# Row softmax: nine-row tiles in ten buffers, stores issued from ScalarE, rows scaled one by one

## The chip, the cores and the metric

The kernel runs on one core of a Trainium2 chip. The metric is device time in microseconds (us); one profiled execution of each kernel gives a span, which is about 1.9 us shorter than the time (164.57 us against 162.7 us for the kernel before). A core has five instruction streams: VectorE (DVE), ScalarE (ACT), GpSimd (POOL), SyncE (SP, which only issues loads here) and TensorE (not used here). Each works through its own list in order. The page of a profile counts 16 DMA engines on the core, which move the data.

## The reference

16,384 rows of 512 floats, softmax with temperature 0.5 over each row:

```
x_scaled = x / 0.5
x_max = np.max(x_scaled, axis=-1, keepdims=True)
exp_x = np.exp(x_scaled - x_max)
return (exp_x / np.sum(exp_x, axis=-1, keepdims=True)).astype(np.float32)
```

That is 33.55 MB in and 33.55 MB out, with little arithmetic.

## The kernel before

128 partitions take 8 rows each, so a tile has 1024 rows (2 MiB) and there are 16 tiles. The row maximum is found on VectorE, the exponential and the row sum on ScalarE; of the 8 rows, 6 are scaled on VectorE in one instruction and 2 on ScalarE. Loads are issued by SyncE, stores by GpSimd.

```python
    G = 8
    ...
    data = ctx.enter_context(tc.tile_pool(name="data", bufs=8))
    stats = ctx.enter_context(tc.tile_pool(name="stats", bufs=8))
    ...
    for c in range(C):
        xt = data.tile([P, G, D], fp32, name="xt")
        nc.sync.dma_start(out=xt, in_=xr[c])
        negmax = stats.tile([P, G], fp32, name="negmax")
        nc.vector.reduce_max(negmax, xt, axis=AX, negate=True)
        sums = stats.tile([P, G], fp32, name="sums")
        for g in range(G):
            nc.scalar.activation(out=xt[:, g, :], in_=xt[:, g, :], func=EXP,
                                 bias=negmax[:, g : g + 1], scale=2.0,
                                 accum_out=sums[:, g : g + 1])
        recip = stats.tile([P, G], fp32, name="recip")
        nc.vector.reciprocal(recip, sums)
        ...   # rows 2 to 7: one tensor_mul on VectorE; rows 0 and 1: COPY with scale on ScalarE
        nc.gpsimd.dma_start(out=outr[c], in_=xt)
```

The library's scheduler decides, when the program is built, in which order the instructions stand on each engine. It keeps the data dependences, not the order of the source.

The softmax here doesn't subtract the row's maximum and nothing guards it: scores larger than these inputs give would overflow.

## Time and profile before

| | before |
|---|---|
| time, median of runs | 164.57 us (164.56 to 164.75, 3 runs) |
| span of the profiled run | 162.7 us |
| DMA over the span | 67.13 MB, 413 GB/s |
| VectorE, ScalarE busy | 77%, 69% |

First the page of the kernel before: busy time of each engine, then 40 equal slices of the span (4.07 us each; a digit is the busy share in tenths, GB/s is what the DMA engines moved), then the chain of work that ended last.

```profile
DVE 124.6 (77%) x48; ACT 112.5 (69%) x289; POOL 8.8 (5%) x20
...
DMA  5999999999999999999999999999999999979994
GB/s 161 431 431 427 431 439 334 411 433 443 423 423 443 431 419 443 439 415 439 443 411 433 443 423 423 443 431 419 439 443 415 435 443 415 431 318 447 407 431 193
...
DMA 61%; DVE 18%; ACT 8%; issue 6%; POOLq 0%; SPq 0%
...
L51 ACT ACTIVATE xt<-xt,negmax 128x512 f32<-128x512 f32 x128 | 90.5, 708 | 28.3 <-DVE negmax L47 28.3
L47 DVE TENSOR_REDUCE negmax<-xt 128x8 f32<-128x4096 f32 x16 | 70.5, 4406 | 25.6 <-DMA xt<-in_x_dram 25.6
L65 DVE TENSOR_TENSOR xt<-xt,recip 128x3072 f32<-128x3072 f32 x16 | 53.6, 3349 | 0.1
```

No engine is near full, the DMA row is full nearly everywhere, and DMA is 61% of the chain. Data movement bounds this kernel. In the lines of groups the two numbers after the bar are total busy us and mean ns of one; after the second bar stands the idle time before them and what ended it: VectorE's reductions wait for loads, ScalarE for the reductions. Two slices fall short: 334 GB/s where the first store begins, 318 GB/s near 145 us.

Next the timeline of VectorE in the middle of the kernel before (start, duration, engine, line, operation):

```profile
97.64 4.42 DVE L47 TENSOR_REDUCE negmax<-xt 128x8 f32<-128x4096 f32 x1 [1.91 <-DMA xt<-in_x_dram]
101.98 3.35 DVE L65 TENSOR_TENSOR xt<-xt,recip 128x3072 f32<-128x3072 f32 x1
105.25 0.20 DVE L61 RECIPROCAL recip<-sums 128x8 f32<-128x8 f32 x1
107.34 4.42 DVE L47 TENSOR_REDUCE negmax<-xt 128x8 f32<-128x4096 f32 x1 [1.90 <-DMA xt<-in_x_dram]
```

One reduction, one scaling, in turn, 9.7 us a tile: for every tile that is loaded one is stored.

### The profile page before, as it was taken

How to read it: one execution, taken by the hardware profiler on the slowest of the kernel's cores; microseconds unless marked ns; L12 is line 12 of the kernel's file. 1: busy time of each engine (PE TensorE's matmuls, PEld its weight loads, DVE VectorE, ACT ScalarE, POOL GpSimd, SP SyncE). 2: the span in 40 equal slices, each digit the busy share in tenths (PEclk: the TensorE clock that was granted, in tenths of full speed). 3: DMA queues.
4: the chain of work that ended last, by engine and by line, in shares of the span. 5: the costliest groups of instructions: out<-in, count | busy, mean ns of one | idle time of the engine just before them, and what ended most of it. 6: DMA issues, size and time to landing. Idle time of an engine off the chain costs nothing.

```text
span 162.7 us, 483 instructions
## 1 busy us (share of the span) xinstructions
DVE 124.6 (77%) x48; ACT 112.5 (69%) x289; POOL 8.8 (5%) x20
## 2 busy tenths in 40 slices
DVE  0098799999999979596993959969596895999200
ACT  0038997999999995939589294885939579396000
POOL 0000010010101010101001010010101001011100
DMA  5999999999999999999999999999999999979994
GB/s 161 431 431 427 431 439 334 411 433 443 423 423 443 431 419 443 439 415 439 443 411 433 443 423 423 443 431 419 439 443 415 435 443 415 431 318 447 407 431 193
DMA packets 4610, 67.13 MB, mean 413 GB/s; under 512 B 512, under 2 KB 512, under 8 KB 512
## 3 DMA queue, kind: packets, MB, share of 16 engines
q1 hardware_dynamic: 2304, 33.56, 49.2%
q0 software_dynamic: 2304, 33.56, 48.3%
q14 instruction: 2, 0.02, 0.0%
HBM read 33.55 MB, written 33.55 MB: 413 GB/s over the span
## 4 chain that ended last, share of the span: by engine, by line
DMA 61%; DVE 18%; ACT 8%; issue 6%; POOLq 0%; SPq 0%
DMA xt<-in_x_dram 40%; DMA out_dram<-xt 22%; DVE negmax L47 11%; ACT xt L51 7%; DVE xt L65 6%; ACT xt L71 1%; DVE recip L61 0%; POOLq L104 0%; SPq L44 0%; POOLq L78 0%
## 5 line engine op out<-in xcount | busy, mean ns | idle before, releaser
L51 ACT ACTIVATE xt<-xt,negmax 128x512 f32<-128x512 f32 x128 | 90.5, 708 | 28.3 <-DVE negmax L47 28.3
L47 DVE TENSOR_REDUCE negmax<-xt 128x8 f32<-128x4096 f32 x16 | 70.5, 4406 | 25.6 <-DMA xt<-in_x_dram 25.6
L65 DVE TENSOR_TENSOR xt<-xt,recip 128x3072 f32<-128x3072 f32 x16 | 53.6, 3349 | 0.1
L51 ACT ACTIVATION_READ_ACCUMULATOR xt<-xt,negmax 128x1 f32 x128 | 24.0, 187 | 0.0
L71 ACT ACTIVATE xt<-xt,recip 128x512 f32<-128x512 f32 x32 | 21.1, 707 | 0.3 <-DVE recip L61 0.3
L78 POOL DMA_DIRECT2D out_dram<-xt x16 | 8.6, 540 | 143.5 <-ACT xt L51 89.3
L51 ACT ACT_TABLE_LOAD x1 | 1.3, 1283 | 8.4 <-DMA xt<-in_x_dram 8.4
L61 DVE RECIPROCAL recip<-sums 128x8 f32<-128x8 f32 x16 | 3.1, 195 | 1.2 <-ACT xt L51 1.2
L93 POOL MEMSET const-float32-0.0<- 128x1 f32 x1 | 0.1, 98 | 0.2 <-issue 0.2
L93 POOL MEMSET const-bfloat16-1.0<- 128x1 bf16 x1 | 0.1, 101 | 0.0
L93 POOL MEMSET const-float32-1.0<- 128x1 f32 x1 | 0.1, 98 | 0.0
L93 POOL MEMSET const-uint8-127<- 128x1 uint8 x1 | 0.1, 98 | 0.0
## 6 DMA issues: line engine op xcount, KB each, us to landing
xt<-in_x_dram SPq DMA_DIRECT2D x16, 2048.0 KB, 28.8
out_dram<-xt POOLq DMA_DIRECT2D x16, 2048.0 KB, 17.0
```

Source lines behind the costliest of these rows:

```text
L47: nc.vector.reduce_max(negmax, xt, axis=AX, negate=True)
L51: nc.scalar.activation(out=xt[:, g, :], in_=xt[:, g, :], func=EXP, bias=negmax[:, g : g + 1], scale=2.0, accum_out=sums[:, g : g + 1],)
L61: nc.vector.reciprocal(recip, sums)
L65: nc.vector.tensor_mul(xt[:, k:, :], xt[:, k:, :], recip[:, k:].unsqueeze(2).broadcast_to((P, G - k, D)),)
L71: nc.scalar.activation(out=xt[:, g, :], in_=xt[:, g, :], func=COPY, scale=recip[:, g : g + 1],)
L78: nc.gpsimd.dma_start(out=outr[c], in_=xt)
L93: nc = _bacc.Bacc("TRN2", target_bir_lowering=False, num_devices=1)
```

## The change

The intent: fewer and larger transfers (15 tiles; 9 rows are an 18 KiB piece of HBM for each partition), more of them in flight (ten buffers), a short last tile (2 rows) for a short end, a simpler split of work (ScalarE only exponentials, VectorE all scaling, row by row, in an instruction form that was expected to be faster), and stores from a hardware queue instead of GpSimd's software queue.

```diff
-    G = 8
-    C = N // (P * G)
+    GMAX = 9
+    R = N // P
+    sizes = [GMAX] * (R // GMAX)
+    if R % GMAX:
+        sizes.append(R % GMAX)
 ...
-    data = ctx.enter_context(tc.tile_pool(name="data", bufs=8))
-    stats = ctx.enter_context(tc.tile_pool(name="stats", bufs=8))
+    data = ctx.enter_context(tc.tile_pool(name="data", bufs=10))
+    stats = ctx.enter_context(tc.tile_pool(name="stats", bufs=4))
+    warm = stats.tile([P, 1], fp32, name="warm", bufs=1)
+    nc.vector.memset(warm, 0.0)
+    nc.scalar.activation(out=warm, in_=warm, func=EXP)   # loads the exponential's table early
 ...
-        nc.vector.reduce_max(negmax, xt, axis=AX, negate=True)
+        nc.vector.tensor_reduce(negmax, xt, axis=AX, op=mybir.AluOpType.max, negate=True)
+        bias = stats.tile([P, G], fp32, name=f"bias{G}")
+        nc.vector.tensor_scalar_mul(bias, negmax, 2.0)
 ...
-        if N_ACT_NORM < G: ... tensor_mul of rows 2 to 7 on VectorE
-        for g in range(N_ACT_NORM): ... COPY with scale of rows 0 and 1 on ScalarE
-        nc.gpsimd.dma_start(out=outr[c], in_=xt)
+        for g in range(G):
+            nc.vector.tensor_scalar_mul(xt[:, g, :], xt[:, g, :], recip[:, g : g + 1])
+        nc.scalar.dma_start(out=outr, in_=xt)
```

More of the change, by code (lines that the diff above doesn't have):

```diff
@@ L19 @@
     P = nc.NUM_PARTITIONS
+    AX = mybir.AxisListType.X
+    EXP = mybir.ActivationFunctionType.Exp
     D = x.shape[-1]
@@ L24 @@
     N = xf.shape[0]
-    G = 8
-    C = N // (P * G)
-    assert C * P * G == N
-    N_ACT_NORM = 2
-    xr = xf.rearrange("(c p g) d -> c p g d", p=P, g=G)
-    outr = of.rearrange("(c p g) d -> c p g d", p=P, g=G)
-    data = ctx.enter_context(tc.tile_pool(name="data", bufs=8))
-    stats = ctx.enter_context(tc.tile_pool(name="stats", bufs=8))
-    AX = mybir.AxisListType.X
-    EXP = mybir.ActivationFunctionType.Exp
-    COPY = mybir.ActivationFunctionType.Copy
-    for c in range(C):
-        xt = data.tile([P, G, D], fp32, name="xt")
-        nc.sync.dma_start(out=xt, in_=xr[c])
-        negmax = stats.tile([P, G], fp32, name="negmax")
-        nc.vector.reduce_max(negmax, xt, axis=AX, negate=True)
-        sums = stats.tile([P, G], fp32, name="sums")
+    GMAX = 9
[3 more added lines that the diff above has]
+        sizes.append(R % GMAX)
+    assert sum(sizes) * P == N
+    data = ctx.enter_context(tc.tile_pool(name="data", bufs=10))
[3 more added lines that the diff above has]
+    nc.scalar.activation(out=warm, in_=warm, func=EXP)
+    row = 0
+    for G in sizes:
+        xr = xf[row : row + P * G, :].rearrange("(p g) d -> p g d", g=G)
+        outr = of[row : row + P * G, :].rearrange("(p g) d -> p g d", g=G)
+        row += P * G
+        xt = data.tile([P, G, D], fp32, name=f"xt{G}", bufs=10 if G == GMAX else 1)
+        nc.sync.dma_start(out=xt, in_=xr)
+        negmax = stats.tile([P, G], fp32, name=f"negmax{G}")
+        nc.vector.tensor_reduce(negmax, xt, axis=AX, op=mybir.AluOpType.max, negate=True)
+        bias = stats.tile([P, G], fp32, name=f"bias{G}")
+        nc.vector.tensor_scalar_mul(bias, negmax, 2.0)
+        sums = stats.tile([P, G], fp32, name=f"sums{G}")
         for g in range(G):
@@ L54 @@
                 func=EXP,
-                bias=negmax[:, g : g + 1],
+                bias=bias[:, g : g + 1],
                 scale=2.0,
@@ L58 @@
             )
-        recip = stats.tile([P, G], fp32, name="recip")
+        recip = stats.tile([P, G], fp32, name=f"recip{G}")
         nc.vector.reciprocal(recip, sums)
-        if N_ACT_NORM < G:
-            k = N_ACT_NORM
-            nc.vector.tensor_mul(
-                xt[:, k:, :],
-                xt[:, k:, :],
-                recip[:, k:].unsqueeze(2).broadcast_to((P, G - k, D)),
-            )
-        for g in range(N_ACT_NORM):
-            nc.scalar.activation(
-                out=xt[:, g, :],
-                in_=xt[:, g, :],
-                func=COPY,
-                scale=recip[:, g : g + 1],
-            )
-        nc.gpsimd.dma_start(out=outr[c], in_=xt)
+        for g in range(G):
+            nc.vector.tensor_scalar_mul(xt[:, g, :], xt[:, g, :], recip[:, g : g + 1])
+        nc.scalar.dma_start(out=outr, in_=xt)
 _INS = ['x']
```

## The prediction

> **What bounds it now.** Data movement. The profile's slices show 411 to 447 GB/s from 4 us to 158 us, except two dips (334 and 318 GB/s); 67.1 MB over the 162.7 us span is 413 GB/s. One load plus one store takes 9.71 us (spacing of the VectorE reductions late in the timeline) = 432 GB/s. VectorE is busy 77%, ScalarE 69%; both wait for loads in mid-kernel. The chain of waits is 61% DMA. What isn't streaming: about 3 us of start, about 1 us lost at the first store, about 1.2 us near 145 us when stores come one by one, and about 2 us of end. So about 5 us at most can be won, by better feeding.
>
> **What the change does, costed.**
> - VectorE: the reduction grows from 4.42 us (8 rows) to about 4.95 (9). Scaling 6 rows in one 3.35 us tensor_tensor becomes 9 one-row tensor_scalar. The Trainium skill, "VectorE: DVE Perf Modes", section "The perf-mode tier table", gives fp32 tensor_scalar twice the rate of tensor_tensor (1227 ns for 2048 elements); my estimate from it for 512 is 0.42 us alone, 0.35 back to back, so 3.1 us for nine. Total VectorE work: about 120 us, little changed.
> - ScalarE loses 32 scaling passes (21.1 us) and gains 15 store issues, estimated at 0.1 to 0.5 us each (load issues take 0.35). The table load moves earlier; it was already hidden.
> - Stores leave the software queue. The Trainium skill, "DMA: Bandwidth & Descriptors", section "Issuing engines are not separate DMA queues", says all issuers share the same engines, so I expect no rate gain; loads and stores split the 432 GB/s evenly in this trace too. It should save the dip at the first store (about 1 us).
> - 18 KiB pieces instead of 16: no rate change expected.
>
> **The main effect: the instruction order.** The built order of the changed kernel is no longer one reduction, one scaling. VectorE reduces tiles 10, 11 and 12 before it scales tile 6, and 14 and 15 before it scales tile 8. Load 12 waits for store 2. ScalarE, which now issues the stores in order, stands still at store 6 until that scaling is done, and its exponentials stand still with it. Adding the trace's durations along this order (5.46 us per 2.25 MiB at 432 GB/s, halves when loads and stores overlap): load 12 lands near 96 us, store 6 is issued near 105, all loads have landed by about 110, store 8 is issued near 122. Eight tiles' stores remain, only seven of them full, with nothing to overlap: each needs nine exponentials (9 x 0.704 = 6.34 us) and an issue, 6.4 to 6.9 us on ScalarE, against 5.46 us of data movement. The queues run dry for about 4 us near 120 to 124 us and 1 to 1.4 us after each later store: about 12 us idle in all, against about 1 before.
>
> **Predicted:** 175 us, range 169 to 179. Faster by over 2%: 0.03; within 2%: 0.10; slower by over 2%: 0.87.
>
> **What would show it.** Slices full until about 110 us, then GB/s near 340 to 370 to the end; ScalarE waiting for VectorE's scaling before stores 3 to 8 (longest wait over 10 us, near store 6), then busy without gaps from about 122 us; ScalarE's last full tiles 6.4 to 6.9 us apart; tensor_scalar near 0.42 us each; row stores landing in the tail about 6.7 us apart.
>
> **What would make it wrong.** Loads taking more than half of the bandwidth beside hardware-queue stores (store 8 earlier: about 6 us less); scaling at single rate, 0.6 us a row (about 15 us more); a store issue on ScalarE hidden or much dearer than 0.4 us (2 us either way); a real gain in rate from 18 KiB pieces.

## The result, and the profile after

The changed kernel takes 176.1 us (176.04 to 176.17, 4 runs) against 164.56 us (164.41 to 164.75, 4 runs): a ratio of 1.0709, with a 95% interval of 1.0688 to 1.073. Ratios here are the mean time of one kernel's runs over that of the other's of the same rounds, so not quite the ratio of the quoted medians. It is slower by 7%.

The page of the changed kernel, the same parts as above (a slice is 4.35 us here):

```profile
DVE 125.3 (72%) x174; ACT 93.5 (54%) x258; POOL 0.2 (0%) x4
...
DMA  6999999999999999999999999959097798798796
GB/s 186 419 453 419 419 457 318 432 432 449 413 436 436 415 438 432 432 441 419 436 436 419 436 432 415 451 229 407 0 436 311 339 407 339 339 407 339 339 407 256
...
DMA 39%; DVE 31%; ACT 21%; issue 3%; ACTq 0%; DVEq 0%; SPq 0%
...
L60 ACT ACTIVATE xt<-xt,bias 128x512 f32<-128x512 f32 x128 | 90.5, 708 | 68.2 <-DVE xt L72 39.2
L54 DVE TENSOR_REDUCE negmax<-xt 128x9 f32<-128x4608 f32 (+1 forms) x15 | 70.4, 4700 | 22.1 <-DMA xt<-in_x_dram 22.1
L72 DVE TENSOR_SCALAR xt<-xt,recip 128x512 f32<-128x512 f32 x128 | 52.0, 480 | 0.2
```

VectorE's total is the same as before and ScalarE has 19 us less to do, yet the kernel is slower. Up to about 110 us the DMA rows of both kernels look alike. After that the changed kernel has a slice of 0 and then a pattern of 339, 339, 407. The chain has moved from DMA to VectorE and ScalarE. The next two windows of the trace say how much that is (length, busy time of VectorE, ScalarE and GpSimd, clock, DMA share, GB/s). First the kernel before:

```profile
4.00:110.00 106.00, 89.14 (x34) 83.24 (x215) 5.45 (x10) 1.00 1.01 427
110.00:161.00 51.00, 35.44 (x15) 29.24 (x74) 3.19 (x6) 1.00 0.98 416
```

And the changed kernel:

```profile
4.00:110.00 106.00, 85.61 (x85) 48.24 (x134) 0.00 (x0) 1.00 1.01 427
110.00:173.00 63.00, 39.64 (x89) 43.79 (x122) 0.00 (x0) 1.00 0.80 337
```

At 110 us both have moved the same bytes at 427 GB/s. Both then have 21.2 MB left (51 x 416 and 63 x 337). At the 432 GB/s of the steady state that takes 49.1 us: the kernel before loses 1.9 us on it, the changed one 13.9 us. The difference, 12.0 us, accounts for the loss of the change (the spans differ by 11.4 us).

What differs at 110 us is *which* bytes have moved. The queues up to that time (packets, MB, share), the kernel before, loads first, then stores:

```profile
q1 hardware_dynamic: 1937, 28.33, 61.7%
q0 software_dynamic: 1200, 17.56, 37.3%
```

The changed kernel, loads first, then stores:

```profile
q1 hardware_dynamic: 2160, 33.56, 72.8%
q10 hardware_dynamic: 749, 12.33, 26.1%
```

The changed kernel has loaded everything and stored little more than a third. From here it can only store, as fast as tiles become ready. Why the stores fell behind stands in VectorE's timeline of the changed kernel:

```profile
76.99 3.65 DVE L72 TENSOR_SCALAR xt<-xt,recip 128x512 f32<-128x512 f32 x9
80.56 4.95 DVE L54 TENSOR_REDUCE negmax<-xt 128x9 f32<-128x4608 f32 x1
87.94 4.95 DVE L54 TENSOR_REDUCE negmax<-xt 128x9 f32<-128x4608 f32 x1 [2.44 <-DMA xt<-in_x_dram]
98.14 4.95 DVE L54 TENSOR_REDUCE negmax<-xt 128x9 f32<-128x4608 f32 x1 [5.25 <-DMA xt<-in_x_dram]
...
103.25 3.65 DVE L72 TENSOR_SCALAR xt<-xt,recip 128x512 f32<-128x512 f32 x9
```

Between the scaling of tile 5 (76.99 us) and that of tile 6 (103.25 us) stand three reductions, of tiles 10, 11 and 12, and two of them wait for their loads. (Pairs of reductions stand ahead of the scalings of tiles 2, 3 and 4 too, and ScalarE has waited 6.57, 11.91 and 7.10 us at stores 3, 4 and 5 before that.) ScalarE has the store of tile 6 in its own list, ahead of the rest of tile 8's exponentials, and stands still with it (ACTq lines are ScalarE issuing a store):

```profile
80.67 0.34 ACTq L74 DMA_DIRECT2D out_dram<-xt  x1
...
106.94 0.34 ACTq L74 DMA_DIRECT2D out_dram<-xt  x1
107.32 0.72 ACT L60 ACTIVATE xt<-xt,bias 128x512 f32<-128x512 f32 x1 [13.46 <-DVE recip L70]
...
125.49 0.34 ACTq L74 DMA_DIRECT2D out_dram<-xt  x1
...
132.07 0.34 ACTq L74 DMA_DIRECT2D out_dram<-xt  x1
...
138.65 0.34 ACTq L74 DMA_DIRECT2D out_dram<-xt  x1
```

No store was issued for 26 us, and ScalarE idled 13.46 us of them in one piece. The label of that wait, a reciprocal on VectorE, names only the nearest event: the store was issued at 106.94 us, just as the scaling of tile 6 ended (103.25 + 3.65 = 106.90). From store 8 at 125.49 us on, stores come every 6.58 us. In that time ScalarE does nine exponentials (nine times 0.704 us, the spacing of their starts, is 6.34 us) and issues a store. A full tile's store needs 5.46 us of data movement at 432 GB/s. So the DMA engines idle between stores.

### The profile page after: what moved, and what is told of

The parts are those of the page before. It is cut to its first block, busy times and chain, and to the rows that moved or that the text cites. A ratio compares the mean times of both kernels' runs of the same rounds, so it can differ in the third digit from the quotient of the medians.

```text
span 174.1 us, 533 instructions
## 1 busy us (share of the span) xinstructions
DVE 125.3 (72%) x174; ACT 93.5 (54%) x258; POOL 0.2 (0%) x4
## 3 DMA queue, kind: packets, MB, share of 16 engines
q1 hardware_dynamic: 2160, 33.56, 46.0%
q10 hardware_dynamic: 2160, 33.56, 45.3%
## 4 chain that ended last, share of the span: by engine, by line
DMA 39%; DVE 31%; ACT 21%; issue 3%; ACTq 0%; DVEq 0%; SPq 0%
DMA xt<-in_x_dram 30%; ACT xt L60 21%; DVE negmax L54 18%; DVE xt L72 13%; DMA out_dram<-xt 9%; DVE recip L70 1%; ACTq L74 0%; DVE bias L56 0%; DVEq L100 0%; SPq L51 0%
## 5 line engine op out<-in xcount | busy, mean ns | idle before, releaser
L60 ACT ACTIVATE xt<-xt,bias 128x512 f32<-128x512 f32 x128 | 90.5, 708 | 68.2 <-DVE xt L72 39.2
L54 DVE TENSOR_REDUCE negmax<-xt 128x9 f32<-128x4608 f32 (+1 forms) x15 | 70.4, 4700 | 22.1 <-DMA xt<-in_x_dram 22.1
L72 DVE TENSOR_SCALAR xt<-xt,recip 128x512 f32<-128x512 f32 x128 | 52.0, 480 | 0.2
L60 ACT ACTIVATION_READ_ACCUMULATOR xt<-xt,bias 128x1 f32 x128 | 23.9, 187 | 0.0
L70 DVE RECIPROCAL recip<-sums 128x9 f32<-128x9 f32 (+1 forms) x15 | 3.1, 207 | 17.3 <-ACT xt L60 17.3
L56 DVE TENSOR_SCALAR bias<-negmax 128x9 f32<-128x9 f32 (+1 forms) x15 | 2.2, 148 | 0.2
```

What stands on the lines that cost most here:

```text
L54: nc.vector.tensor_reduce(negmax, xt, axis=AX, op=mybir.AluOpType.max, negate=True)
L56: nc.vector.tensor_scalar_mul(bias, negmax, 2.0)
L72: nc.vector.tensor_scalar_mul(xt[:, g, :], xt[:, g, :], recip[:, g : g + 1])
```

## The experiments

Three explanations were set against each other. **The theory**: the built order of VectorE's instructions (groups of reductions ahead of a scaling) lets late loads hold back the stores, and since the stores stand in ScalarE's list, ScalarE loses its lead too; the loss is paid in a store-only tail at ScalarE's pace. **Rival 1**: issuing stores from ScalarE, or from a hardware queue, is itself the cost. **Rival 2**: the new sizes and forms are the cost (18 KiB pieces, the odd last tile, one-row scalings).

Each run was timed beside runs of the kernel before on the same chip. R10 below means the reduction of tile 10 on VectorE, S6 the scaling of tile 6. The built orders were read from the programs (dots: the pattern goes on):

```
changed kernel : R1 R2 S1 R3 R4 S2 R5 R6 S3 R7 R8 S4 R9 S5 R10 R11 R12 S6 R13 S7 R14 R15 S8 S9 ... S15
e1, edges added: R1 R2 S1 R3 S2 R4 S3 R5 S4 R6 S5 R7 S6 R8 S7 R9 S8 R10 S9 ... R15 S14 S15
kernel before  : R1 R2 S1 R3 R4 S2 R5 S3 R6 S4 R7 S5 R8 S6 R9 S7 R10 S8 ... R16 S14 S15 S16
```

So "plain" (one reduction, one scaling) is not one order. When a tile is scaled, the reductions are one tile ahead in e1, two in the kernel before, e2, e7 and e11, three in e12, and up to seven in the changed kernel (R15 before S8).

### e1: the same instructions in another order

```diff
-        nc.vector.tensor_reduce(negmax, xt, ...)
+        if len(scaled) >= 2:                      # LAG = 2 in the file, written out here
+            with tc.issue_after(scaled[-2]):      # stands behind that scaling; no wait is added
+                nc.vector.tensor_reduce(negmax, xt, ...)
+        else:
+            nc.vector.tensor_reduce(negmax, xt, ...)
 ...
+        scaled.append(last.ins)                   # the tile's last scaling instruction
```

> The changed kernel, same instructions, same queues, same tiles; only issue-order edges on VectorE hold each reduction behind the scaling two tiles earlier, so that the reductions of tiles 10 to 12, and 14 to 15, no longer stand before the scalings of tiles 6 and 8. Theory (the order couples the stores to loads that land late, and leaves a store-only tail at ScalarE's pace): about 164.5 us (range 163 to 167), no store waiting over 5 us on ScalarE, DMA at 430 GB/s until past 145 us. Rival 1 (issuing stores from ScalarE's in-order queue is itself the cost): stays near 176. Rival 2 (18 KiB pieces, hardware queue for stores, or one-row scalings are slower): stays near 176.

Measured: 163.48 us (163.36 to 163.69, 4 runs), ratio to before 0.9941 (0.9906 to 0.9975). The slices of e1:

```profile
DMA  6999999999999999999999999999999999999993
GB/s 187 424 429 424 433 424 429 328 438 426 429 433 440 429 433 433 433 433 420 429 429 433 429 438 438 435 424 438 433 429 424 429 437 416 430 438 429 438 438 153
```

The pattern at the end is gone, the rate holds until the last slice. Tiles, buffers, queues and instruction forms are those of the changed kernel, so neither rival by itself can be the cause of the loss. Two things should be known about e1. Its edges undo the earlier pairs of reductions as well as the group of three: store 5, which stands before that group, was issued at 60.76 us in e1 and at 80.67 us in the changed kernel. And ScalarE's list was rebuilt too: store 6 follows six exponentials of tile 7 in e1, two of tile 8 in the changed kernel. One detail was expected wrongly: that no store would wait over 5 us. VectorE's timeline of e1 has the scaling of tile 6, and ScalarE's the stores of tiles 6 and 8 (here ACTq, L81), each holding ScalarE up:

```profile
65.95 3.65 DVE L78 TENSOR_SCALAR xt<-xt,recip 128x512 f32<-128x512 f32 x9
...
78.20 0.34 ACTq L81 DMA_DIRECT2D out_dram<-xt  x1
78.58 0.72 ACT L66 ACTIVATE xt<-xt,bias 128x512 f32<-128x512 f32 x1 [8.34 <-DMA xt<-in_x_dram]
...
100.05 0.34 ACTq L81 DMA_DIRECT2D out_dram<-xt  x1
100.44 0.72 ACT L66 ACTIVATE xt<-xt,bias 128x512 f32<-128x512 f32 x1 [6.19 <-DMA xt<-in_x_dram]
```

What they waited for was not their own scaling (that of tile 6 ended at 65.95 + 3.65 = 69.60 us, 8.6 us before its store) but the landing of a *load*. The built program has the reason: eight completion counters serve loads and stores together, and store 6 has to wait until the load that used its counter last has landed. In e1 these waits, 19.0 us in three (stores 6, 8 and 9), cost nothing that can be seen, because the DMA engines stayed full throughout.

### e2 and e3: stores on GpSimd, in the plain and in the grouped order

```diff
# e2 (the scheduler then builds the plain order by itself)
-        nc.scalar.dma_start(out=outr, in_=xt)
+        nc.gpsimd.dma_start(out=outr, in_=xt)
# e3: as e2, with each VectorE instruction pinned to the order of the changed kernel
+        keep = tc.keep_in_program_order
+        # steps traced in the order R1 B1 R2 B2 S1 ... S5 R10 R11 R12 B10 S6 ... (B: bias and exponentials)
```

> The changed kernel with the stores back on GpSimd; nothing else edited, but the scheduler then builds the plain order (one reduction, one scaling) by itself. Theory: about 164.5 us (163 to 166.5). Rival 1: also about 164.5. Rival 2 (piece size, one-row scalings): stays near 176. A further rival from the Trainium skill (VectorE's two-port mode keeps GpSimd from writing descriptors): some us above 165, stores starting late.

> Stores on GpSimd, but VectorE's instructions pinned to the order that the scheduler built for the changed kernel. ScalarE is then free of stores. Theory that both parts are needed (late loads hold the scalings, AND ScalarE stands still with the store): about half of the loss, 169.5 us (167 to 172); DMA dry for about 6 us between 109 and 127 us, none in the tail because the exponentials ran ahead. Order alone: 176. Rival 1 (only ScalarE's queue matters): 164.5.

Measured: e2 164.99 us (ratio 1.003, 0.9995 to 1.0065), e3 171.34 us (ratio 1.0427, 1.0382 to 1.0472). With e1 and the changed kernel this makes a square:

| VectorE's order | stores from ScalarE | stores from GpSimd |
|---|---|---|
| plain | 163.48 us (e1) | 164.99 us (e2) |
| grouped | 176.1 us (the change) | 171.34 us (e3) |

The order alone costs 6.4 us where GpSimd stores (171.34 - 164.99) and 12.6 us where ScalarE does (176.1 - 163.48). Moving the stores to ScalarE costs nothing in the plain order and 4.8 us in the grouped one. Both parts of the theory are needed. The plain row mixes two orders (one tile ahead in e1, two in e2); e11 below has the reductions two tiles ahead and ScalarE's stores, at 164.57 us, and with it in the place of e1 the order costs 11.5 us and the reading is the same. A caveat on e3: only VectorE's order was pinned; the order of ScalarE's exponentials follows the traced steps. Windows of e3 show the dry stretch and, after it, a tail that is no longer at ScalarE's pace:

```profile
110.00:128.00 18.00, 17.86 (x33) 12.52 (x35) 1.07 (x2) 1.00 0.62 265
128.00:168.00 40.00, 21.66 (x59) 14.50 (x42) 3.74 (x7) 1.00 0.98 412
```

The further rival in e2's text rests on the Trainium skill, "SBUF — State Buffer", section "Who interferes with whom". The total of e2 speaks against it, but hardly tests it: in e2 only one of the 15 store issues ran while VectorE was scaling. In e3 seven did, and each of these issues is recorded with 533 to 541 ns, as those beside a reduction did (533 ns, the first 667).

### e4: the kernel before, one word changed

```diff
-        nc.gpsimd.dma_start(out=outr[c], in_=xt)
+        nc.scalar.dma_start(out=outr[c], in_=xt)
```

> The kernel before with one word changed: stores issued from ScalarE. Eight buffers, 16 KiB pieces, block scaling, two rows scaled on ScalarE, all as before. The scheduler then groups VectorE's reductions (three before the scaling of tile 3, three before that of tile 5) here too. Adding the trace's durations along the built order: about 200 us (190 to 210), DMA first dry near 82 us, 4 us at a time. Rival 2 (the piece size or one-row scalings are the cause): near 164.5.

Measured: 199.64 us (199.05 to 200.06), ratio 1.2135. VectorE's timeline of e4 shows three reductions in a row before the scaling of the third tile (x2 stands for two), the third of them waiting for its load:

```profile
34.62 8.74 DVE L47 TENSOR_REDUCE negmax<-xt 128x8 f32<-128x4096 f32 x2
47.57 4.42 DVE L47 TENSOR_REDUCE negmax<-xt 128x8 f32<-128x4096 f32 x1 [4.22 <-DMA xt<-in_x_dram]
...
52.13 3.36 DVE L65 TENSOR_TENSOR xt<-xt,recip 128x3072 f32<-128x3072 f32 x1
```

The mechanism needs no nine-row tile and no one-row scaling; it came with the one word. With eight buffers and two scalings left on ScalarE it costs three times as much as in the change. So the other parts of the change together softened it; how much each did is not shown, and the groups stand earlier here too (R5 R6 R7 before S3).

### e5 and e6: the dip at the first store, and e1 again

```diff
     nc.scalar.activation(out=warm, in_=warm, func=EXP)
+    nc.scalar.dma_start(out=of[N - P : N, 0:1], in_=warm)   # e5: e1 with an early small store
```

> The ordered kernel of e1 with one extra small store (128 x 4 bytes) from ScalarE at the start, into rows that the last tile overwrites. In the kernel before, in the changed one and in e1 the DMA rate falls to about 355 GB/s between 25 and 30 us and to about 420 in the next 5 us, when the first store begins, and never again so. If that is a cost of the store queue's first use, it moves to the start, where little else runs: about 162.4 us (162.0 to 162.9), no dip near 28 us. If it is a cost of turning from loads to loads and stores: dip and time as e1, 163.5.

> The kernel of e1 again, beside e5 and with more rounds, as its yardstick and to settle whether it beats the kernel before: 163.5 us, ratio 0.990 to 0.997.

Measured: e5 163.38 us (ratio 0.9939, 0.9919 to 0.9958), e6 163.42 us (ratio 0.994, 0.9921 to 0.9958). The dip stayed. The window of e5 where the first large store begins:

```profile
25.00:35.00 10.00, 9.93 (x15) 7.84 (x23) 0.00 (x0) 1.00 1.00 387
```

e1 has 389 GB/s in the same window, the kernel before 387, the changed one 389. So a store queue's first use is not the cause, at least not one that a 128 x 4 byte store can take away; what is stays open. (The windows give 338 to 350 GB/s between 25 and 30 us for those three kernels and 428 to 437 in the next 5 us, so the figures in e5's text are a little off.) The packets of the kernel before show where the time goes: load packets (of over 4 KB) that start between 26 and 27 us take 1112 ns on average against 611 ns between 20 and 24 us, and the first packet of the store, issued at 22.82 us, is recorded only at 27.77 us. e6 settles that the ordered form of the change beats the kernel before, by 0.6%.

### e7: one-row scalings in the kernel before

```diff
-        if N_ACT_NORM < G: ... one tensor_mul of rows 2 to 7
-        for g in range(N_ACT_NORM): ... rows 0 and 1 on ScalarE
+        for g in range(G):
+            nc.vector.tensor_scalar_mul(xt[:, g, :], xt[:, g, :], recip[:, g : g + 1])
```

> The kernel before with the scaling of all eight rows one by one on VectorE (tensor_scalar), none on ScalarE; stores stay on GpSimd. The data movement bounds, so theory: within 1% of before, 164 to 166 us. Rival 2 (one-row scalings cost time, or their two-port mode starves GpSimd's store descriptors): clearly slower, 168 us or more.

Measured: 163.79 us (163.52 to 164.15), ratio 0.9966 (0.9942 to 0.999). The scaling form costs nothing, as long as DMA bounds. GpSimd's store issues took as long as before (540 ns on average in both), but this says little about the second half of rival 2 (the page is named under e2): only two of the 16 issues ran while VectorE was scaling. Those two took 531 ns, like most.

### e8, e9, e10: single parts of the change undone, order left to the scheduler

```diff
# e8
-    GMAX = 9
+    GMAX = 8
# e9
-        for g in range(G): ... tensor_scalar_mul of one row
+        nc.vector.tensor_mul(xt, xt, recip.unsqueeze(2).broadcast_to((P, G, D)))
# e10
-    data = ctx.enter_context(tc.tile_pool(name="data", bufs=10))
+    data = ctx.enter_context(tc.tile_pool(name="data", bufs=8))   # and bufs=8 for xt
```

> The changed kernel with eight rows a tile (16 KiB pieces, sixteen equal tiles, no two-row tile), all else as changed; the built order still has three reductions before the scaling of tile 6. Theory (order): about 176 us (174 to 178), as the changed kernel. Rival 2 (18 KiB pieces or the odd last tile are the cost): back towards 165.

> The changed kernel with one tensor_tensor for all nine rows in place of nine one-row tensor_scalar; same groups of reductions in the order. A tile's scaling takes about 5.0 us instead of 3.6. Since VectorE's reductions and scalings are on the chain in the middle of this kernel, theory: slower than the changed kernel, about 181 us (179 to 184). Rival 2 (the one-row form is what made it slow): faster than 176.

> The changed kernel with eight buffers instead of ten. The same grouped reductions then wait for loads whose buffers come free later: theory about 186 us (182 to 190). If ten buffers are what made it slow (loads run too far ahead and leave a store-only tail): faster than 176.

Measured: e8 177.34 us, e9 179.84 us, e10 185.56 us (each within 0.4 us over 4 runs). None gets near 165. In e8 the scheduler grouped three reductions before S6 again, with 16 KiB pieces and no short tile. e9 is 3.7 us slower than the change: VectorE is on the chain here, and the block form took 4.86 us a tile against 3.57 us (the spacing from the start of the scaling to the next instruction). That this is the whole reason is not shown, for e9's built order differs a little: R15 stands after S8. e10 shows that ten buffers help the grouped order rather than cause it: a reduction that stands too early waits for a load, and with fewer buffers that load comes later (R14 waits 8.94 us for its load and store 8 is issued at 134.50 us, against no such wait and 125.49 us in the change).

### e11 and e12: how far ahead may a reduction stand?

The edit is that of e1 with LAG = 3 and 4 in place of 2, written out again:

```diff
-        if len(scaled) >= 2:
-            with tc.issue_after(scaled[-2]):
+        if len(scaled) >= 3:                      # e12: 4
+            with tc.issue_after(scaled[-3]):      # e12: -4
```

> As e1, but each reduction is held behind the scaling three tiles earlier, one more tile of slack than e1. Theory: each further reduction that goes ahead of a scaling delays the stores, so that more of them are left when the loads end, and that tail runs at ScalarE's 6.6 us a tile instead of 5.5: about 164.7 us (163.5 to 166), DMA nearly full to the end. If the slack does not matter and only the triple group did: 163.4 as e1.

> As e1 with four tiles of slack. Theory: about 168.3 us (166.5 to 170), DMA first short near 137 us and then by about 1.1 us a tile. If only the triple group mattered: 163.4 as e1.

Measured: 164.57 us with three (ratio 1.0031, 1.0007 to 1.0056), 168.33 us with four (ratio 1.0258, 1.0232 to 1.0284), after 163.4 us with two. There is no triple group in any of these, so the group of three is not the whole cause: in these runs the loss grows with how far ahead the reductions stand. LAG = 2, 3 and 4, which let the reductions stand one, two and three tiles ahead, give ratios to the kernel before of 0.994 (e6), 1.0031 and 1.0258; the changed kernel, with up to seven, gives 1.0709. No run holds the group of three alone. Each further reduction ahead leaves more stores for the end, as the last slices of e12 show:

```profile
GB/s 186 425 433 425 429 429 402 367 425 425 435 438 433 433 429 435 433 425 425 429 433 433 433 438 429 438 431 425 425 429 419 443 282 354 283 425 354 283 425 267
```

## Why the prediction was right

The prediction said 175 us in a range of 169 to 179; it is 176.1 us. Point by point:

- *What bounds the kernel before*: data movement. Right (though the lowest slice outside the two dips is 407 GB/s, not 411), and e7 confirms it: 21 us taken off ScalarE and the scaling rearranged moved the time by 0.3%.
- *The order as main effect*: right. e1 changes nothing but the order and takes the whole loss away; e3 brings a bit more than half of it back (171.34 against 164.56 us), without ScalarE's part.
- *The times along the chain*: load 12 near 96 us (its reduction starts at 98.14), store 6 near 105 (106.94), all loads landed by about 110 (all 33.56 MB moved at 110), store 8 near 122 (125.49), later stores 6.4 to 6.9 us apart (6.58). The trace's durations, added along the built order, were enough. ScalarE waited before each of stores 3 to 8, as predicted, longest before store 6 (13.46 us), and was busy without gaps from store 8 to its last exponential.
- *About 12 us idle against about 1*: measured as 13.9 us against 1.9 us of lost data movement after 110 us. The difference was right, both were a little larger.
- *The cost of a one-row scaling*: undersized. I estimated 0.42 us alone and 3.1 us for nine from the page's 2048-element figure; it took 0.48 us and 3.57 us for nine. Over the three scalings between load 12 and store 8 this makes 1.4 of the 3.5 us by which store 8 came later than predicted; the rest is load 12, about 2.1 us late.
- *The total*: its closeness is partly luck. Store 8 came 3.5 us late, but the time from there to the end of the span was 48.6 us (174.1 - 125.49), where the prediction left about 51 (175, less 2 for the span, less 122). The two errors nearly cancel.
- *Store issues on ScalarE, 0.1 to 0.5 us*: each shows 0.34 us, of which 0.24 us lengthen the tile (6.58 - 6.34).
- *The hardware queue would save the dip at the first store, about 1 us*: wrong. The dip is there with either queue (387 and 389 GB/s between 25 and 35 us).
- *No rate change from 18 KiB pieces, loads and stores splitting the rate evenly*: right. 427 GB/s in both kernels up to 110 us; while both queues moved data between 30 and 110 us, by the packet records, loads had 212 and stores 218 GB/s in the changed kernel (214 and 217 in the kernel before). The skill's statement quoted in the prediction, that the issuing engine gives no other DMA engines, agrees with this; what that section does not speak of is that the work behind a store in the issuer's list waits with it.

What remains open: why the scheduler builds the grouped order. In both pairs that differ only in this (the kernel before and e4; e2 and the changed kernel) the grouped order came with stores from ScalarE and the plain one with stores from GpSimd. No run isolates the scheduler's reason. The shared completion counters that e1 shows held up no store of the changed kernel from store 2 to store 9: each was issued within 0.04 us of the end of its own scaling. Whether they delayed its loads stays open.

## What to carry to other kernels

When a kernel is bound by data movement, do not only ask whether the DMA engines are busy, ask whether loads and stores advance together: bytes loaded too early leave a tail of stores that runs at the pace of compute. A scheduler's order can decide that, so read the built order of every engine after moving an instruction from one queue to another, above all a store into the list of an engine that computes, and add durations along it. If a reduction of a later tile stands ahead of the scaling of an earlier one, an edge that only fixes the order (e1) is cheap to try; here it turned a 7% loss into a 0.6% gain.

## What the Trainium skill lacked or had wrong

- "VectorE: DVE Perf Modes", section "The perf-mode tier table (the rule you actually need)", gives fp32 tensor_scalar for 2048 elements only (1227 ns, twice the rate of tensor_tensor). My estimate for 512 elements from it was 0.42 us; one with a per-partition scalar took 0.480 us, and 0.397 us from start to start (3.57 us for nine). The faster rate for rows of 512 does show: nine rows took 3.57 us against 4.86 us as one tensor_tensor of nine rows (e9), a gain of 1.4. That does not contradict the factor of 2, which compares single instructions of equal size; no run here has that pair.
- "SBUF — State Buffer", section "Who interferes with whom", says that VectorE's two-port modes, which tensor_scalar can enter, keep GpSimd from the port with which it writes store descriptors. With 128 such scalings and all stores on GpSimd (e7) no loss was seen: 163.79 us against 164.41 us. That is no contradiction, since only two of e7's 16 store issues ran beside a scaling; but in e3 seven of 15 did, and none of these took longer than 541 ns, against 533 ns beside a reduction. The page does not say for which transfers it matters; here each full store was 2 to 2.25 MiB.
- "DMA: Bandwidth & Descriptors" names no cost where the first store joins a stream of loads. The six traces compared show a dip there: 385 to 401 GB/s between 25 and 35 us (before 387, changed 389, e1 389, e2 385, e5 387, e7 401) against some 430 before and after, with both kinds of queue, and not taken away by a small early store.
- "DMA: Bandwidth & Descriptors", section "Issuing engines are not separate DMA queues", does not warn that a store issued by an engine that computes holds that engine's later work until the stored data is ready: 13.46 us in one piece here. The premise stands elsewhere on the page, under "Anatomy of one DMA — SWDGE (gpsimd) path": a wait for a semaphore happens on the sequencer that issues, before the transfer is handed on.
